# A hybrid attention / DeltaNet / MLP layer: eight modulation rows formed in the MLP stage instead of the output projection, and three query tiles transposed inside the attention

## Chip, cores and metric

The kernel runs on one core of a Trainium2 chip. The metric is the device time of one execution in microseconds (us), taken as the median of several runs. Lower is better.

## What is computed

The reference is one layer of a diffusion backbone for 512 latent tokens (width 1024) with 256 context tokens in front of them. Only the latent stream is returned.

```python
mod_lat = silu(c) @ w_mod + b_mod                      # six rows of 1024: sh1, sc1, g1, sh2, sc2, g2
hx = modulate(rms_norm(x), sh1, sc1)                   # and hc from the context, with its own rows
... = split_cols(hx @ w_in)                            # attention q, k, v; DeltaNet q, k, v; gates
attn_x = latent_attention(q_x, [k_c, k_x], [v_c, v_x]) # 8 query heads, 2 key heads, head width 128
gdn_x  = gdn_output(gdn_bidirectional(...), z_x)       # chunked gated DeltaNet, both directions
x = x + g1 * ((sigmoid(g_a) * (attn_x @ w_pa) + sigmoid(g_d) * (gdn_x @ w_pd)) @ w_out)
x = x + g2 * conv_ffn(modulate(rms_norm(x), sh2, sc2)) # up 1024 -> 5632, conv of width 3, gate, down
return rms_norm(x, final_norm_w)
```

`g2` scales the MLP's output alone, so nothing reads it before the first column block of the down projection is finished.

## The kernel before

Every large product is done in three TensorE passes: both operands are split into a rounded part and the rest (`whi`, `wlo` for weights, `...H`, `...L` for activations), and `mm3` issues hi·hi, hi·lo and lo·hi. So each weight tile of 512 KB is loaded (`load_w`, L205, on the DMA queue of the sync engine, SP), rounded on ScalarE (ACT, L118, tile `whi`) and subtracted on VectorE (DVE, L106, tile `wlo`). `load_w` has two buffers for the raw tile and three each for `whi` and `wlo`.

The stages follow each other on TensorE (PE):

1. Modulation rows sh1 and sc1, normalised inputs, then the attention's k, v and q projections, block by block (`blk`, six of them). A q tile of 128 tokens x 256 columns (two heads) is accumulated in a PSUM tile `pq`, rotated (`rope`, on DVE, which reads `pq`) into an SBUF tile `qt`, and later transposed by `columns` (L89, PSUM tile `pt`, two buffers) into QH (ACT) and QL (DVE). `columns` runs `LAG` = 3 tiles behind the projection, through the list `pend`; the tiles left in `pend` after the last block are transposed in a loop behind it.
2. The attention (`attend`), which goes over 32 pairs of head and token tile. For each it computes scores into the PSUM tile `pS`, the softmax, the transposes of the probabilities (`ab`), and for every second pair the product with the values. Between these steps it takes steps from a generator of projections for the DeltaNet (`fillA`, matmuls into `mb`). A finished projection is transposed by `tokens` through `xbank`, a single PSUM tile named `xb`: ACT copies it out and then takes squares of it in place.
3. The DeltaNet, woven with further projections, with the projection by `w_pa` of the attention's output and, last, with the projection by `w_pd` of the DeltaNet's output. For each of the eight column blocks c, `finish_pd` loads two stored tiles (`gd` and `ga`, L1234 and L1236, two buffers each), multiplies the block's PSUM bank into `gd` on DVE (L115), adds `ga` on GpSimd (POOL, L106), and writes the result to yH (ACT) and yL (DVE, L115, both named `y`).
4. The output projection, `out_proj`: eight column blocks c, each 24 matmuls over k = 0..7 of yH and yL, into PSUM tiles `mc`. Block c = 0 needs the eighth y tile at its last three matmuls.
5. `normed` forms the second normalised input h2 by halves of the tokens, between matmuls; then 44 blocks of the up projection (`up`, `up_finish`), the down projection, and the last normalisation (`emit`, tile `ot`).

`late_mods` is a generator that forms the other four modulation rows g1, sh2, sc2 and g2, 32 steps of 128 entries each. A step loads one 512 KB tile of `w_mod` (L381, tile `wl`, two buffers) and multiplies it on DVE by silu(c), `cw`, with a sum along the row (L382); every eight steps a small add puts eight columns into `mod`. `more_mods(rate)` takes the next step whenever the rates add up to one: 0.25 per k in `w_pa` (MPA), 0.14 in `w_pd` (MPD), 0.25 in `out_proj` (MPO). That is 16 steps in the first, 8 in the second, and the last 8, which are g2, in `out_proj`.

The order on PE is the program's (`pinned[0]` holds it there). On the other engines a scheduler puts instructions in order by priority (`first()`, `sooner()`) and by its own estimate of when they can start, so instructions of a later stage can stand ahead of earlier ones. An engine, and SP's DMA queue too, then works strictly in that order: an instruction that waits holds up all behind it.

Of the kernel before, what the change touches and what calls it, by code (L numbers as in the profile page):

```python
# [45 lines left out]
PMB = 1  # L46
XV, YV = 4, 0
NS = 2
MPA, MPD, MPO = .25, .14, .25
DA = '203242'  # L50
DAT = [(int(DA[i]), int(DA[i + 1])) for i in range(0, len(DA), 2)]
KPIN, LAG, FQ = 1, 3, 0
# [24 lines left out]
def hybrid_layer_body(tc, x, ctxt, xT, consts, cols, rows, w_mod1, w_mod2, w_av, w_aq, w_cm, w_pa, w_pd, w_out,  # L77
# [39 lines left out]
    def act(out, a, f=AF.Copy, **kw):  # L117
        A.activation(out, a, f, **kw)  # L118
# [13 lines left out]
    with es:  # L132
# [61 lines left out]
        def xbank():  # L194
            return xps.tile([P, 4, P], F32, name="xb", tag="x")
# [171 lines left out]
        def late_mods():  # L367
            cw = lmp[0].tile([P, D], F32, name="cw")
            ms = lmp[0].tile([P, 32], F32, name="ms")

            def row():
                return lmp[0].tile([P, D], F32, name="wl", tag="wl", bufs=2)

            SP.dma_start(cw, rows[R_C:R_END].partition_broadcast(P))
            th = row()
            act(th, cw, AF.Tanh, scale=0.5)
            stt(cw, th, 1.0, cw, ALU.add, ALU.mult)
            yield
            for j in range(32):
                wl = row()  # L380
                SP.dma_start(wl, w_mod2[j])  # L381
                tc.keep_in_program_order(V.scalar_tensor_tensor(out=wl, in0=wl, scalar=0.5, in1=cw, op0=ALU.mult, op1=ALU.mult,  # L382
                                                                accum_out=ms[:, j:j + 1]))
                if j % 8 == 7:
                    tt(mod[:, 9 + j:17 + j], ms[:, j - 7:j + 1], col[:, S_BMOD + 9 + j:S_BMOD + 17 + j], ALU.add)
                yield

        lm_es, lmp, mods, mcount = ExitStack(), [], late_mods(), [0.0]

        def more_mods(rate):  # L390
            mcount[0] += rate
            while mcount[0] >= 1:
                mcount[0] -= 1
                next(mods, None)
# [253 lines left out]
        with kv_es:  # L648
# [16 lines left out]
                        tt(o5[:, :, hf, :], s5[:, :, 1 - hf, :], b4[:, :, hf, :], ALU.mult)  # L665
                tt(out, out, tmp, ALU.add)

            def columns(blk, t, qt):
                pt = kps.tile([P, 2, P], F32, name="pt", tag="pt", bufs=2)
                for j in range(2):  # L670
                    transpose(pt[:, j, :], qt[:, j * 128:j * 128 + 128])
                ts_ = slice(t * P, t * P + P)
                hi, lo = (KH, KL) if blk == 0 else (QH[blk - 2], QL[blk - 2])
                split(hi[:, :, ts_], lo[:, :, ts_], pt)
# [4 lines left out]
            for blk in range(6):  # L679
# [5 lines left out]
                for t in range(6 if blk < 2 else 4):  # L685
# [14 lines left out]
                    if blk == 1:  # L700
                        split(VH[:, t, :], VL[:, t, :], pq[:, 0:256])
                        V.tensor_copy(psc[:, t, :], pq[:, 256:288])
                        continue
                    qt = kvp.tile([P, 256], F32, name="qt", tag="qt", bufs=LAG + 1)
                    tmp = kvp.tile([P, 256], F32, name="qtmp", tag="qtmp", bufs=2)
                    if blk == 0:
                        ss = kvp.tile([P, 2], F32, name="kss", tag="kss", bufs=2)
# [21 lines left out]
            chunk[0] = 1  # L729
            for i in range(FQ):  # L730
                next(fillA, None)
            while pend:
                columns(*pend.pop(0))
            pinned[0] = False
        tb_es.close()

# [1 line left out]
        with at_es:  # L738
# [63 lines left out]
            def attend():  # L802
                U = 4 * NH
                at = lambda u: (u // 4, u % 4)
                pS, pms, pv = scores(0, 0), {}, None
                yield F0
                for u in range(U + 2):
                    if u < U:
                        pms[u] = softmax(*at(u), pS)
                    if u + 1 < U:  # L810
                        pS = scores(*at(u + 1))
                    yield F1
                    nxt = None
                    if 0 < u <= U:
                        nxt = probs(*at(u - 1), pms.pop(u - 1))
                    yield F2
                    if pv is not None:
                        pv()
                    yield F3
                    pv = nxt  # L820
# [508 lines left out]
        with ExitStack() as fe:  # L1329
# [40 lines left out]
            def out_proj(c, w, cols):  # L1370
                po = m2bank()[:, cols]
                for k in range(KT):
                    ks = slice(k * P, k * P + P)
                    mm3(po, w[0][:, ks], w[1][:, ks], yt[0][:, k, cols], yt[1][:, k, cols], k, KT)
                    more_mods(MPO)
                with first():
                    stt(x1[c][:, cols], po, mod[:, 16 + c:17 + c], x1[c][:, cols], ALU.mult, ALU.add)

# [65 lines left out]
                            normed(1, token_rows(rc))  # L1444
            for ci in ups[:UH]:
                up_finish(ci)
            for ci in ups[UH:]:
                up(ci, load_w(w_up[ci]), slice(0, NL))
                up_finish(ci)
            pinned[0] = False  # L1450

            fnw = lambda c: col[:, S_FNW + c:S_FNW + c + 1]
# [14 lines left out]

            def emit(i, pr):
                h = half(i)
                ot = fs.tile([P, KT, HT], F32, name="ot", tag="ot")  # L1470
                for j in (KT - 1, *range(KT - 1)):
                    if j == KT - 1:
                        stt(ot[:, j, :], x1[j][:, h], fnw(j), pr, ALU.mult, ALU.mult)
                    else:
                        tt(ot[:, j, :], x1[j][:, h], pr, ALU.mult)
                for (c0, n) in ((KT - 1, 1), (0, 3), (3, 2), (5, 2)):
                    SP.dma_start(outT[c0:c0 + n, :, h].rearrange("c p n -> p c n"), ot[:, c0:c0 + n, :])
# [103 lines left out]
```

## Time and profile before

| | us |
|---|---|
| median of 3 runs | 1266.66 |
| the three runs | 1260.86, 1266.66, 1273.11 |
| the profiled execution, its own time | 1263.61 |
| its span in the trace | 1261.8 |
| PE busy | 1197.7 (95% of the span) |
| DVE busy | 837.8 (66%) |
| ACT busy | 614.1 (49%) |

All times inside the program are counted from the start of the span. The q projections end at about 151 us, the attention runs from there to about 320 us, the DeltaNet with the projections woven into it to about 834 us, the output projection to about 885 us, and the MLP to the end. A busy PE can run at full clock or at half of it; the column PEclk gives the granted clock of a stretch as a share of 2.4 GHz.

### The profile page before, as it was taken

To read this page: it belongs to the slowest core of one execution; us is meant where nothing else is said; L and a number is where in the kernel's file an instruction comes from. 1 tells how busy PE (TensorE), PEld (TensorE's weight loads), DVE (VectorE), ACT (ScalarE), POOL (GpSimd) and SP (SyncE) were. 2 spreads that over 40 slices of the span, in tenths; PEclk is the share of its full clock that TensorE was granted. 3 is DMA by queue.
4 is the path that set the end of the run, shared out by engine and by line. 5 is a ranking of instruction groups with operands and counts; after the bars stand their busy time and mean duration, and the time that the engine had idled before them with its cause. 6 is when DMAs were issued, how large, how long until landed. Compare 5 with 4: busy or idle time off the path is not lost.

```text
span 1261.8 us, 20507 instructions
## 1 busy us (share of the span) xinstructions
PE 1197.7 (95%) x7733; PEld 1017.9 (81%) x7733; DVE 837.8 (66%) x1608; ACT 614.1 (49%) x1402; POOL 276.9 (22%) x347
## 2 busy tenths in 40 slices
PE   7999899999878999999999989899999999999997
PEld 4599889899767788778888778679988888888886
DVE  5667767777699866866657777866765566653333
ACT  6534476666766663763635532223544444442231
POOL 0030110110432496596484100220000000000000
PEclk8999999999999999999999999989999999999998
DMA  9312311121636434444436776883133332233331
GB/s 380 138 59 84 103 42 68 71 76 59 204 110 196 158 126 141 137 146 141 147 124 206 260 262 203 270 309 117 51 100 100 100 101 94 90 96 95 102 93 67
DMA packets 66323, 171.31 MB, mean 136 GB/s; under 512 B 7376, under 2 KB 18096, under 8 KB 64816
## 3 DMA queue, kind: packets, MB, share of 16 engines
q1 hardware_dynamic: 66224, 170.00, 40.4%
q8 instruction: 61, 1.00, 0.3%
q14 instruction: 38, 0.31, 0.1%
HBM read 144.75 MB, written 25.21 MB: 135 GB/s over the span
## 4 chain that ended last, share of the span: by engine, by line
PE 72%; DVE 9%; DMA 8%; POOL 4%; ACT 4%; issue 3%; SPq 0%; POOLq 0%; DVEq 0%; ACTq 0%
PE mc L85 32%; PE mb L85 17%; PE pq L85 6%; PE pb L85 5%; PE pS L85 3%; PE ab L85 3%; DMA wl<-in_w_mod_dram 2%; DVE wlo L106 2%; PE pm L85 2%; PE ab L89 2%; DMA Gb<-gamdr 1%; POOL prod L106 1%; POOL R L106 1%; POOL NN L106 1%; PE pk L85 1%
## 5 line engine op out<-in xcount | busy, mean ns | idle before, releaser
L106 DVE TENSOR_TENSOR wlo<-wraw,whi 128x1024 fp32r<-128x1024 f32 (+1 forms) x153 | 192.7, 1260 | 159.1 <-ACT whi L118 158.2
L118 ACT ACTIVATE whi<-wraw 128x1024 fp32r<-128x1024 f32 (+1 forms) x153 | 159.7, 1044 | 215.0 <-PE mc L85 109.0
L85 PE MATMUL mc<-h,whi 128*128 128x512 f32 (+1 forms) x752 | 219.7, 376 | 0.3 <-ACT whi L118 0.3
L85 PE MATMUL mb<-hxH,whi 128*128 128x512 f32 x384 | 161.4, 420 | 5.4 <-DVE t L115 2.7
L85 PEld LDWEIGHTS mc<-h,whi 128*128 128x128 f32 x752 | 138.0, 188 | 26.1 <-ACT whi L118 0.5
L85 PE MATMUL mb<-hxH,wlo 128*128 128x512 f32 x384 | 151.3, 394 | 0.0
L85 PE MATMUL mb<-hxL,whi 128*128 128x512 f32 x384 | 150.8, 393 | 0.0
L85 PE MATMUL mc<-h,wlo 128*128 128x512 f32 (+1 forms) x376 | 141.3, 376 | 0.5 <-DVE wlo L106 0.5
L85 PE MATMUL mc<-a,whi 128*128 128x512 f32 (+1 forms) x396 | 111.1, 366 | 0.6 <-DVE x L115 0.6
L106 POOL TENSOR_TENSOR rc<-rc,mhalf 128x2 f32<-128x2 f32 x4 | 3.0, 745 | 411.5 <-DVE rc L112 411.5
L85 PEld LDWEIGHTS mb<-hxH,wlo 128*128 128x128 f32 x384 | 72.5, 189 | 16.6
L85 PEld LDWEIGHTS mb<-hxH,whi 128*128 128x128 f32 x384 | 72.9, 190 | 15.8 <-issue 3.6
L85 PEld LDWEIGHTS mc<-a,whi 128*128 128x128 f32 x396 | 71.5, 189 | 12.8 <-DVE x L115 0.8
L85 PEld LDWEIGHTS mc<-h,wlo 128*128 128x128 f32 x376 | 70.8, 188 | 13.6 <-DVE wlo L106 1.0
L85 PEld LDWEIGHTS mb<-hxL,whi 128*128 128x128 f32 x384 | 73.1, 190 | 9.6
L85 PE MATMUL mc<-a,wlo 128*128 128x512 f32 (+1 forms) x198 | 72.3, 365 | 0.0
L115 DVE SCALAR_TENSOR_TENSOR u<-mc,col,u 128x511 f32<-128x511 f32 x88 | 65.3, 746 | 1.4
L106 POOL TENSOR_TENSOR R<-R,prod 128x31 f32<-128x31 f32 (+15 forms) x93 | 58.1, 625 | 7.0
L106 POOL TENSOR_TENSOR prod<-X,R 128x31 f32<-128x31 f32 (+15 forms) x93 | 53.3, 573 | 19.9 <-DVE X L106 13.2
L85 PE MATMUL pq<-whi,hxH 128*128 128x256 f32 (+1 forms) x192 | 55.4, 288 | 0.0
L85 PE MATMUL pq<-wlo,hxH 128*128 128x256 f32 (+1 forms) x192 | 54.1, 282 | 0.0
L85 PE MATMUL pq<-whi,hxL 128*128 128x256 f32 (+1 forms) x192 | 54.0, 281 | 0.0
(323 smaller groups left out, 2768.5 us busy)
## 6 DMA issues: line engine op xcount, KB each, us to landing
wraw<-in_w_cm_dram SPq DMA_DIRECT2D x48, 512.0 KB, 3.5
wraw<-in_w_up_dram SPq DMA_DIRECT2D x44, 512.0 KB, 3.3
wl<-in_w_mod_dram SPq DMA_DIRECT2D x32, 512.0 KB, 4.6
wm<-in_w_mod_dram SPq DMA_DIRECT2D x8, 1024.0 KB, 10.3
wraw<-in_w_down_dram SPq DMA_DIRECT2D x16, 512.0 KB, 3.5
wraw<-in_w_aq_dram SPq DMA_DIRECT2D x10, 512.0 KB, 4.2
M<-gamdr SPq DMA_DIRECT2D x64, 64.0 KB, 4.8
wraw<-in_w_pa_dram SPq DMA_DIRECT2D x8, 512.0 KB, 4.6
```

Source lines behind the costliest of these rows:

```text
L85: i = nc.tensor.matmul(*a, **k)
L89: i = nc.tensor.transpose(*a, **k)
L106: (eng or V).tensor_tensor(out=out, in0=a, in1=b, op=op)
L115: V.scalar_tensor_tensor(out=out, in0=a, scalar=s, in1=b, op0=op0, op1=op1)
L118: A.activation(out, a, f, **kw)
```

## The change

Three edits. First, `late_mods` stops after 24 steps, and `out_proj` takes none. The last eight are formed by a new generator, `gate_mods`, in the first MLP stage: it loads c once more (`cw2`), forms silu(c) in two instructions (a tanh on ACT, an `stt` on DVE), then loads the rows two at a time (1 MB each) into the tile `ot`, which `emit` uses at the very end, and multiplies them on DVE, two instructions for each load. It is stepped after every up block with an odd index. Second, `columns` accepts a PSUM tile from outside; the loop that emptied `pend` behind the q projections is gone, and `attend` transposes one of the three remaining q tiles in each of its first three rounds, through `xbank`. Third, `qt` moves to the pool that lives through the attention, and `ot` takes the shape of two rows.

```diff
-MPA, MPD, MPO = .25, .14, .25
+MPA, MPD = .25, .14
@@ late_mods
-            for j in range(32):
+            for j in range(24):
                 wl = row()
...
+        def gate_mods(pool, fs):
+            two_rows = lambda: fs.tile([P, 2, D], F32, name="wl2", tag="ot")
+            cw = pool.tile([P, D], F32, name="cw2")
+            ms = pool.tile([P, 8], F32, name="ms2")
+            SP.dma_start(cw, rows[R_C:R_END].partition_broadcast(P))
+            th = two_rows()
+            act(th[:, 0], cw, AF.Tanh, scale=0.5)
+            stt(cw, th[:, 0], 1.0, cw, ALU.add, ALU.mult)
+            yield
+            for j in range(0, 8, 2):
+                wl = two_rows()
+                SP.dma_start(wl, w_mod2[24 + j:26 + j].rearrange("j p d -> p j d"))
+                yield
+                for i in range(2):
+                    tc.keep_in_program_order(V.scalar_tensor_tensor(out=wl[:, i], in0=wl[:, i], scalar=0.5, in1=cw, op0=ALU.mult,
+                                                                    op1=ALU.mult, accum_out=ms[:, j + i:j + i + 1]))
+                yield
+            tt(mod[:, 40:48], ms, col[:, S_BMOD + 40:S_BMOD + 48], ALU.add)
@@ columns
-            def columns(blk, t, qt):
-                pt = kps.tile([P, 2, P], F32, name="pt", tag="pt", bufs=2)
+            def columns(blk, t, qt, pt=None):
+                if pt is None:
+                    pt = kps.tile([P, 2, P], F32, name="pt", tag="pt", bufs=2)
@@ the q projections
-                    qt = kvp.tile([P, 256], F32, name="qt", tag="qt", bufs=LAG + 1)
+                    qt = ap_.tile([P, 256], F32, name="qt", tag="qt", bufs=LAG + 1)
...
-            while pend:
-                columns(*pend.pop(0))
             pinned[0] = False
@@ attend
                     yield F1
+                    if pend:
+                        columns(*pend.pop(0), xbank()[:, 0:2, :])
                     nxt = None
@@ out_proj
-                    more_mods(MPO)
@@ the up projection
+            gates = gate_mods(fp, fs)
             for ci in ups[UH:]:
                 up(ci, load_w(w_up[ci]), slice(0, NL))
                 up_finish(ci)
+                if ci % 2:
+                    next(gates, None)
+            for _ in gates:
+                pass
@@ emit
-                ot = fs.tile([P, KT, HT], F32, name="ot", tag="ot")
+                ot = fs.tile([P, 2, D], F32, name="ot", tag="ot").rearrange("p a (b n) -> p (a b) n", n=HT)
```

On PE, at the end of the q projections, the transposes of four q tiles, two each, stand between the last `pq` matmul and the first scores before the change (`pt<-cst,qt`: half a q tile against the identity):

```order
L85 MATMUL pq<-whi,hxL 128x256
L85 MATMUL pq<-wlo,hxH 128x256
L89 MATMUL pt<-cst,qt 128x128 x8
L85 MATMUL pS<-KH,QH_720 128x512
L85 MATMUL pS<-KL,QH_720 128x512
```

Of these eight, two are left there with the change:

```order
L85 MATMUL pq<-whi,hxL 128x256
L85 MATMUL pq<-wlo,hxH 128x256
L89 MATMUL pt<-cst,qt 128x128 x2
L85 MATMUL pS<-KH,QH_720 128x512
L85 MATMUL pS<-KL,QH_720 128x512
```

The other six stand in the first three rounds of the attention. On PE the third of these three tiles is between the transposes of a projection (`xb<-cst,co`) and those of the probabilities (`ab<-cst,pm`), in the same PSUM tile `xb` as the one before it:

```order
L85 MATMUL mb<-hcL,whi 128x256
L85 MATMUL mb<-hcH,wlo 128x256
L89 MATMUL xb<-cst,co 128x128 x2
L89 MATMUL xb<-cst,qt 128x128 x2
L89 MATMUL ab<-cst,pm 128x128 x6
L85 MATMUL mb<-hcH,whi 128x256
```

So the transposes of three tiles moved from a stretch without other matmuls into rounds that have them, and into a bank that others use.

On DVE, where the last `w_pd` blocks end and the output projection begins, before the change (`wl,ms<-wl,cw` is a modulation row, `gd<-gd,mb` and `y<-gd` are the first and last step of `finish_pd`, `x_0<-mc` is the first block of `out_proj`):

```order
L115 SCALAR_TENSOR_TENSOR gd<-gd,mb 128x512 x2
L106 TENSOR_TENSOR wlo<-wraw,whi 128x1024
L382 SCALAR_TENSOR_TENSOR wl,ms<-wl,cw 128x1024
L115 SCALAR_TENSOR_TENSOR y_9122<-gd,y_9122 128x512
L382 SCALAR_TENSOR_TENSOR wl,ms<-wl,cw 128x1024
L115 SCALAR_TENSOR_TENSOR y_9122<-gd,y_9122 128x512
L106 TENSOR_TENSOR wlo<-wraw,whi 128x1024
L382 SCALAR_TENSOR_TENSOR wl,ms<-wl,cw 128x1024
L115 SCALAR_TENSOR_TENSOR gd<-gd,mb 128x512
L382 SCALAR_TENSOR_TENSOR wl,ms<-wl,cw 128x1024
L115 SCALAR_TENSOR_TENSOR gd<-gd,mb 128x512
L106 TENSOR_TENSOR wlo<-wraw,whi 128x1024
```

The same place with the change:

```order
L115 SCALAR_TENSOR_TENSOR gd<-gd,mb 128x512
L106 TENSOR_TENSOR wlo<-wraw,whi 128x1024
L115 SCALAR_TENSOR_TENSOR y_9122<-gd,y_9122 128x512 x2
L106 TENSOR_TENSOR wlo<-wraw,whi 128x1024
L115 SCALAR_TENSOR_TENSOR gd<-gd,mb 128x512
L115 SCALAR_TENSOR_TENSOR y_9122<-gd,y_9122 128x512
L115 SCALAR_TENSOR_TENSOR gd<-gd,mb 128x512
L106 TENSOR_TENSOR wlo<-wraw,whi 128x1024
L115 SCALAR_TENSOR_TENSOR y_9122<-gd,y_9122 128x512
L115 SCALAR_TENSOR_TENSOR x_0_9495<-mc,mod,x_0_9495 128x512
```

The rows between the steps of `finish_pd` are gone, and of its last two blocks, c = 6 now finishes (`y`) ahead of the first step of c = 7.

On SP's DMA queue the 44 loads of the up projection stood in one piece before. With the change c (`cw`) and the four pairs of rows (`wl`, 128x2x1024) stand among them:

```order
L205 DMA wraw<-in_w_up_dram 128x1024 x5
L393 DMA cw_10224<-in_rows_dram 128x1024
L400 DMA wl_10339<-in_w_mod_dram 128x2x1024
L205 DMA wraw<-in_w_up_dram 128x1024 x8
L400 DMA wl_10491<-in_w_mod_dram 128x2x1024
L205 DMA wraw<-in_w_up_dram 128x1024 x4
L400 DMA wl_10643<-in_w_mod_dram 128x2x1024
L205 DMA wraw<-in_w_up_dram 128x1024 x4
L400 DMA wl_10795<-in_w_mod_dram 128x2x1024
L205 DMA wraw<-in_w_up_dram 128x1024 x23
```

Each pair's load has to wait until the pair ahead of it, in the same single tile, has been multiplied, and the weight loads behind it wait with it. On DVE the first pair's two multiplications stand between the eleventh and the twelfth `wlo` of the up projection, and each further pair four `wlo` later. On ACT the tanh of c stands between the sixth and the seventh tile of `normed`'s first half, ahead of the first Silu of the MLP.

## Rows read from the trace of the kernel before

**Rows 1.** The profile page's section 1 (busy us, share of the span, instructions) and the engines' shares of the chain that ended last.
```profile
PE 1197.7 (95%) x7733; PEld 1017.9 (81%) x7733; DVE 837.8 (66%) x1608; ACT 614.1 (49%) x1402; POOL 276.9 (22%) x347
PE 72%; DVE 9%; DMA 8%; POOL 4%; ACT 4%; issue 3%; SPq 0%; POOLq 0%; DVEq 0%; ACTq 0%
```

**Rows 2.** The timeline of PE where the output projection begins: start us, us, line, operation, tiles, count, and in brackets the idle time before it and what ended it.
```profile
833.70 0.63 PE L85 MATMUL mc<-y,whi 128*128 128x512 f32 x2
...
839.91 0.50 PE L85 MATMUL mc<-y,whi 128*128 128x512 f32 x1 [1.59 <-DVE y L115]
841.66 0.80 PE L85 MATMUL mc<-y,whi 128*128 128x512 f32 x1 [0.77 <-DVE y L115]
...
848.24 0.39 PE L85 MATMUL mc<-y,wlo 128*128 128x512 f32 x1
...
848.92 0.39 PE L85 MATMUL mc<-y,wlo 128*128 128x512 f32 x1
```

**Rows 3.** Stretches of the same place: from:to, length, busy us and instructions of PE, PEld, DVE, ACT, POOL, then PEclk, DMA share, GB/s.
```profile
808.00:812.00 4.00, 1.93 (x9) 1.31 (x8) 2.20 (x4) 1.06 (x1) 1.16 (x1) 1.00 1.05 362
841.00:842.00 1.00, 0.34 (x1) 0.34 (x2) 0.61 (x2) 0.00 (x0) 0.00 (x0) 0.50 1.03 385
847.00:848.00 1.00, 1.00 (x4) 0.80 (x3) 0.00 (x0) 0.00 (x0) 0.00 (x0) 0.64 0.99 401
```

**Rows 4.** The timeline of DVE there, as in rows 2.
```profile
823.06 1.89 DVE L106 TENSOR_TENSOR wlo<-wraw,whi 128x1024 fp32r<-128x1024 f32 x1
824.87 2.31 DVE L382 SCALAR_TENSOR_TENSOR wl<-wl,cw 128x1024 f32<-128x1024 f32 x1
...
827.12 0.68 DVE L115 SCALAR_TENSOR_TENSOR y<-gd,y 128x512 fp32r<-128x512 f32 x1
...
832.83 1.23 DVE L382 SCALAR_TENSOR_TENSOR wl<-wl,cw 128x1024 f32<-128x1024 f32 x1 [2.15 <-DMA wl<-in_w_mod_dram]
...
833.99 0.68 DVE L115 SCALAR_TENSOR_TENSOR gd<-gd,mb 128x512 f32<-128x512 f32 x1
```

**Rows 5.** The other steps of `finish_pd`: two rows of ACT's timeline, and of the view of the tile `gd` (count, min/median/max ns, first and last start) its POOL step and, last, the DMA time from issue to landing.
```profile
823.90 0.63 ACT L118 ACTIVATE y<-gd 128x512 fp32r<-128x512 f32 x1 [0.89 <-POOL gd L106]
826.13 0.63 ACT L118 ACTIVATE y<-gd 128x512 fp32r<-128x512 f32 x1 [1.60 <-POOL gd L106]
L106 POOL TENSOR_TENSOR gd<-gd,ga x8: 1294/2199/2305, 797.6 to 837.1; 128x512 f32<-128x512 f32 x8
DMA to landing us min/median/max: 3.7/5.4/5.8
```

**Rows 6.** The timelines of PE and DVE at the end of the q projections, as in rows 2.
```profile
150.61 0.60 PE L89 MATMUL pt<-cst,qt 128*128 128x128 f32 x4
154.33 0.44 PE L89 MATMUL pt<-cst,qt 128*128 128x128 f32 x2 [3.12 <-DVE QL L106]
155.39 0.78 PE L85 MATMUL pS<-KH,QH 128*128 128x512 f32 x1
153.26 0.60 DVE L106 TENSOR_TENSOR qtmp<-pq,qB 128x64 f32<-128x64 f32 x4
```

**Rows 7.** Stretches of the same place, columns as in rows 3.
```profile
154.00:155.00 1.00, 0.44 (x2) 0.20 (x2) 0.93 (x3) 0.20 (x1) 0.91 (x1) 0.91 0.89 188
157.00:158.00 1.00, 1.00 (x6) 0.90 (x5) 0.30 (x1) 0.00 (x0) 0.00 (x0) 0.50 0.08 16
```

**Rows 8.** The timelines of PE and ACT in the first rounds of the attention, where `xb` is used.
```profile
165.69 0.82 PE L89 MATMUL ab<-cst,pm 128*128 128x128 f32 x6
170.09 0.82 PE L89 MATMUL ab<-cst,pm 128*128 128x128 f32 x6
172.21 0.66 PE L89 MATMUL xb<-cst,co 128*128 128x128 f32 x4 [0.59 <-ACT xb L118]
166.00 0.19 ACT L118 ACTIVATION_READ_ACCUMULATOR xb<-xb 128x1 f32 x1
170.29 0.38 ACT L118 ACTIVATE co<-xb 128x256 f32<-128x256 f32 x1 [1.49 <-PE xb L89]
```

**Rows 9.** The second token sums in `normed`: DVE's scale `rc` and the diagonal `dg`, and PE's use of `dg`.
```profile
889.20 0.16 DVE L112 TENSOR_SCALAR rc<-mc 128x2 f32<-128x2 f32 x1
890.36 0.48 DVE L110 TENSOR_SCALAR dg<-cst,rc 128x128 f32<-128x128 f32 x2 [0.59 <-POOL rc L106]
892.34 0.60 PE L85 MATMUL mc<-dg,cst 128*128 128x128 f32 x4
```

**Rows 10.** The MLP's up projection: a stretch of 40 us (columns as in rows 3), and of the waits from 905 to 1080 us (who waited for whom, us in total, times, longest) two rows.
```profile
920.00:960.00 40.00, 40.00 (x178) 33.14 (x177) 24.06 (x30) 17.79 (x23) 0.00 (x0) 1.00 0.30 99
DVE wlo L106 <- ACT whi L118: 55.4, 32, 4.4
PEld mc L85 <- DVE wlo L106: 1.0, 1, 1.0
```

**Rows 11.** The rows of `w_mod` before: the multiplications on DVE (min/median/max ns), the tanh of c on ACT, and the only load of an activation table from there on.
```profile
L382 DVE SCALAR_TENSOR_TENSOR wl<-wl,cw x32: 1210/1219/2316, 709.6 to 854.6; 128x1024 f32<-128x1024 f32 x32
L118 ACT ACTIVATE wl<-cw x1: 1060/1060/1060, 704.0 to 704.0; 128x1024 f32<-128x1024 f32 x1
907.78 1.28 ACT L118 ACT_TABLE_LOAD   x1 [0.83 <-DVE u L115]
```

## The prediction

> **What bounds the kernel now.** I read the page's busy times and chain first: PE is busy for 95% of the span and holds 72% of the chain that ended last [rows 1]. So an edit pays only where PE waits, or runs at half clock. The timeline of PE around the two places that the change touches shows both. Where the output projection begins, PE waits 1.59 us and 0.77 us for DVE's y tiles and then works at half rate: 16 matmuls from 841.66 to 848.24 took 6.58 us, where three from 848.24 to 848.92 took 0.68 [rows 2]. The granted clock there is 0.50, 1.2 GHz, and back at full before 848 [rows 3]. Where the attention begins, PE waits 3.12 us for DVE, and again works at half clock, from about 154.9 to 158.1 [rows 6, 7]. In the MLP's up projection PE has no wait at all and DVE is busy 24.06 of 40 us [rows 10].
>
> **Part one: eight rows leave the output projection.** Removed are eight loads of 512 KB and eight DVE multiplications of 1.21 us at least and up to 2.32 beside POOL [rows 11]. Only those on the path of the last two y tiles (blocks c = 6 and 7 of w_pd) count. That path runs: y of block 4 frees `gd`, its load is issued, lands a median 5.4 us later, then DVE, POOL (1.3 to 2.3), ACT (0.63), DVE (0.68) [rows 4, 5].
> Before: ACT has the hi part of block 4 at 823.90 + 0.63 = 824.53, but DVE runs a row from 824.87 for 2.31 us, and y follows at 827.12. The load for block 6 comes behind that; a further row at 832.83, itself held 2.15 us by its load, puts block 6's first step at 833.99 [rows 4].
> After, with the rows gone: DVE is free at 823.06 + 1.89 = 824.95, y of block 4 ends at 825.6, that of block 5 (ACT done at 826.13 + 0.63 = 826.76) at 827.5. Loads land at 831.0 and 832.9. Block 6: 0.68 + 1.3 + 0.63 + 0.68 from 831.0 gives 834.4. Block 7 stands behind it on DVE: first step to 835.1, POOL up to 2.3 beside a `wlo`, 837.4, ACT 838.0, DVE 838.7. PE starts block 0 of the output projection at 833.70 [rows 2] and needs block 7 after 21 matmuls of 0.227 us, at 838.5. So of 1.59 + 0.77 = 2.36 us about 0.2 stays: 2.2 us gained.
> The half clock: 16 matmuls at 0.227 us are 3.6, so 6.58 - 3.6 = 2.9 us more. The clock fell after two waits close together. The wait of 2.07 us that ends at 810.86 is in a stretch at granted clock 1.00 [rows 3]. So 0.2 us will not bring it down: 2.9 us gained. Together 5.1. Bounds: at best 5.3 (no wait at all); at worst 0, if block 7 arrives as late as now. I take 5.1, since the path holds 3 us of rows and needs only 2.4 us less. What is late next is nothing on PE for the rest of this projection: since three weight tiles are held ready.
>
> **Part two: the same work in the MLP.** Four loads of 1 MB, one of c, a tanh (1.06 us), an stt, and eight multiplications of 1.22 us [rows 11].
> The tanh and the stt fall into `normed`, ahead of the second `rc`. They delay it by about 0.7 us (the stt begins 0.5 us earlier than `rc` does now and takes 1.2). `dg` is now ready at 890.84 and PE uses it at 892.34 [rows 9]: 1.5 us of cover, so no cost; without the cover up to 1.2 us.
> A pair holds DVE for 2.5 us, once in four up blocks. Its cover: in 40 us DVE is idle for 16, and `wlo` waits 55.4 us in 32 times for ACT's rounding, which waits for a buffer to come free, while PE waited for `wlo` once, 1.0 us [rows 10]. A weight tile is ready some two blocks before PE wants it, so a delay of 2.5 us stays hidden. On SP's queue a pair's load waits for the pair ahead, which DVE finishes before the `wlo` that the next weight load waits for anyway. So 0, with a bound of four pairs times 2.5 = 9.8 us if all of it came through, and none below zero, since PE has no wait there to lose.
> One rule speaks against this part. The only table load after the early tanh at 704 is the 1.28 us at 907.78, ahead of the first Silu [rows 11]. The Trainium skill (ScalarE: Activation LUTs, section "Table sets: the hidden batching unit") says that functions should be grouped by table set, because each change of set costs a load. By that rule a tanh behind the first Silu would bring two more loads, and the sum would be 2.6 us higher; in the order the tanh stands ahead of that Silu, under the set that served the tanh at 704, so the sum takes none.
>
> **Part three: three q tiles transposed inside the attention.** The first scores no longer stand behind six transposes. They wait for the last reader of the `pq` bank that they take over: DVE ends it at 153.26 + 0.60 = 153.86, and PE begins 0.1 us later, where it begins at 155.39 now [rows 6]: 1.4 us earlier. PE's idle time is 2.9 us, hardly shorter than now, so I let the clock fall as it does; as more work then runs at half rate, 1.2 us are left.
> What is added lies in `xb`, a single bank: each pair of transposes (0.24 us) waits until ACT has finished with the tile before. In round 2 PE would be at the transposes of the probabilities at 165.69 - 1.0, while the squares of `xb` end at 166.19, some 0.9 earlier by now: 0.6 us of wait. In round 3 the pair stands directly behind a transpose into the same bank, whose copy begins at 170.29 and is followed by two squares of 0.45 us each [rows 8]: PE stands for 1.5 us, with the probabilities behind it. In return the wait of 0.59 us at 172.21, for those same squares, is gone [rows 8]. Sum: -1.2 + 0.7 + 0.6 + 1.5 - 0.6 = 1.0, of which some 0.6 goes in waits that PE has in these rounds anyway: +0.4 us. Bounds: -3.0, if the clock stays up (1.6 us more) and no wait arises; +2.7, if ACT, which gets three more copies into its fullest rounds, makes the two waits twice as long. I take +0.4, by the order of the rows.
>
> **Sum.** -5.1 + 0 + 0.4 = -4.7 us. The profiled execution took 1263.61 us, which gives 1258.9. It lies 3.05 us below the median of the runs shown, and the runs spread over 12; for a median I add half of that difference: 1260.4 us.
>
> **Rivals.**
> The wait stays (B): block 7 is late for another reason, its load or POOL's add, and PE stands again for 1.5 us and loses its clock. For it: the load's landing takes up to 5.8 us [rows 5], and the x tiles are loaded in the same stretch at a DMA share of 1.03 [rows 3]. Against: these loads are issued two microseconds earlier, before that burst. Gain about 1 us, less 0.4: 1263 us, or 1264.5 as a median.
> The MLP is starved (C, the slower side): the pairs come through to PE. Place: the `wlo` behind each pair; price 2.5 us for each, 9.8 in all; it decides from the point where a weight tile is ready less than 2.5 us ahead of its block. For it: PE did wait for a `wlo` once, at the head of this stage. Against: that was before the three buffers had filled, and none followed [rows 10]. 1258.9 + 9.8 = 1268.7, slower than the profiled execution by 5 us; 1270 as a median.
> The attention keeps its clock (D): an idle time of 2.9 us lies between the 2.07 that did not bring the clock down and the 3.12 that did [rows 3, 6]. Then this part gives up to 3.0 instead of costing 0.4: 1255.5, or 1257 as a median.
>
> **How the numbers follow.** Forecast 0.53, B 0.22, C 0.10, D 0.15. The range: D's 1255.5 less 3 us, as far as the lowest of the runs lies below the profiled one, is 1252.5; C's 1270 and 1 us is 1271. A measurement of this kernel tells about 1% from no change, 12.7 us. Faster by that means under 1254, which only the lower tails of D and of the forecast reach: 0.09. Slower by that needs C together with the bad end of the attention and a half clock in the MLP: 0.04. The rest, 0.87, is the same.
>
> **What would show it.** Right: no `y` wait of over 0.5 us on PE around 834 to 845 and a granted clock of 1.00 there; the first scores about 1.4 us earlier, then a wait of PE of about 1.5 us at the third `xb<-cst,qt`; PE without a wait beside the four pairs; `rc` about 0.7 us later with PE unmoved. Wrong: a wait of PE on `wlo` in the up projection, a half clock at the head of the output projection, a second table load in the MLP, or an attention that ends more than 3 us later or earlier against its beginning than now.

## Result and profile after

| | before | after |
|---|---|---|
| median, us | 1265.78 (1260.86 to 1273.11, 20 runs) | 1259.17 (1254.90 to 1264.39, 20 runs) |
| the profiled execution, us | 1263.61 | 1254.90 |
| its span, us | 1261.8 | 1253.1 |

The ratio is 0.9948 with a 95% interval of 0.9935 to 0.9961: 6.6 us faster, between 4.9 and 8.2. That is a change of less than 1%, to which the prediction gave a chance of 0.87. The time that it forecast, 1260.4 us, is 1.2 above the measured median.

The profile page of the changed kernel, section 1 and the engines' shares of the chain that ended last [rows 1]:

```profile
PE 1193.0 (95%) x7733; PEld 1015.7 (81%) x7733; DVE 834.0 (67%) x1609; ACT 613.8 (49%) x1403; POOL 274.0 (22%) x347
PE 74%; DMA 7%; DVE 6%; POOL 5%; ACT 4%; issue 2%; SPq 0%; POOLq 0%; DVEq 0%; ACTq 0%
```

The work is the same; PE's busy time shrank by 4.7 us, 3.6 of them from 820 to 848 us, since a matmul at half clock counts as busy for longer. The two profiled executions differ by 8.7 us, more than the medians. To see where, the same matmul in PE's order is looked up in both traces, and the table gives by how much a stretch between two such matmuls is longer (+) or shorter (-) than in the trace of before, in us. The bounds are times in the trace of before; the runs are those of the experiments below.

| kernel | 0-150 | 150-200 | 200-330 | 330-395 | 395-760 | 760-820 | 820-848 | 870-890 |
|---|---|---|---|---|---|---|---|---|
| after | +2.3 | +0.24 | 0.0 | -0.6 | -3.9 | -0.3 | -6.43 | 0.0 |
| a2, after again | 0.0 | +0.23 | +0.1 | +0.7 | -0.8 | -0.5 | -6.30 | 0.0 |
| e1, rows only | +1.6 | -0.05 | 0.0 | +3.5 | -0.5 | +0.2 | -6.59 | 0.0 |
| e2, transposes only | +1.9 | +0.22 | 0.0 | +2.8 | -0.8 | -0.4 | -0.81 | 0.0 |
| e4, rows late | +0.1 | 0.0 | +0.1 | +1.4 | -2.0 | +0.5 | -3.08 | +3.70 |
| f0, rows and loads late | +0.1 | 0.0 | +0.1 | +3.5 | -0.1 | 0.0 | -6.54 | +6.63 |
| e8, rows narrow | +0.4 | 0.0 | +0.1 | +3.7 | -0.8 | +0.2 | -4.20 | 0.0 |
| f1, after + two loads | +2.1 | +0.22 | 0.0 | -1.1 | -3.0 | +0.4 | -5.07 | 0.0 |
| f2, after + multiplications | +2.4 | +0.19 | 0.0 | +4.0 | -1.8 | -0.4 | -4.27 | 0.0 |
| e5, other bank | +2.6 | -1.14 | +0.1 | +2.5 | -4.7 | +0.5 | -6.36 | 0.0 |
| e6, clock kept | +1.8 | -0.73 | 0.0 | +3.5 | +1.5 | +2.1 | -6.49 | 0.0 |
| c1, e5 and e6 | +0.2 | -2.04 | 0.0 | +2.2 | -0.6 | +0.5 | -6.54 | 0.0 |
| e7, more MLP work | +2.4 | +0.17 | +0.1 | +2.4 | -3.2 | -0.5 | -6.17 | 0.0 |

From 848 to 870 every run is within 0.01 us of before, and from 890 to 1250 within 0.04; behind that up to 0.5 us is left out here. In the stretches 0-150 and 330-760 PE has the work of before in all of these kernels, and yet they differ by several us. The edits are not the cause of all that: after and a2 are the same program, and differ by 2.3, 1.3 and 3.1 us in 0-150, 330-395 and 395-760; and e1, e4, f0 and e8, in which DVE, ACT and POOL work in the order of before from 330 to 395, are 1.4 to 3.7 us longer there. (In the kernels with the moved transposes a few instructions of DVE and ACT stand in another order in these stretches; what that is worth was not tried.) The stretches that the edits touch are steadier: kernels with the same code agree to 0.2 us from 150 to 200, and the eight without rows and loads at the head of the output projection agree to 0.4 us from 820 to 848. With the stop still there the spread is larger: e2 has the code of before from 820 to 848 and takes 0.81 us less. So effects are read by stretch here, and the change's gain in this one is 6.4 us against the profiled execution of before, 5.6 against e2.

**The output projection.** PE's timeline where it begins (start us, us, line, operation, tiles, count), and a stretch of 11 us (from:to, length, busy us and instructions of PE, PEld, DVE, ACT, POOL, then PEclk, DMA share, GB/s) [rows 2, 3]:

```profile
830.67 0.61 PE L85 MATMUL mc<-y,whi 128*128 128x512 f32 x2
...
834.75 0.62 PE L85 MATMUL mc<-y,whi 128*128 128x512 f32 x2
835.20 0.39 PE L85 MATMUL mc<-y,wlo 128*128 128x512 f32 x1
835.43 0.79 PE L85 MATMUL mc<-y,whi 128*128 128x512 f32 x2
...
839.48 0.39 PE L85 MATMUL mc<-y,wlo 128*128 128x512 f32 x1
```
```profile
834.00:845.00 11.00, 11.00 (x50) 8.86 (x49) 5.62 (x8) 4.99 (x8) 0.27 (x1) 1.00 0.52 173
```

No wait is left and the granted clock is 1.00: from 830.67 to 839.48 it takes 8.8 us, where before the same matmuls (833.70 to 848.24) took 14.5. DVE's timeline behind it, then SP's queue (gd's loads) and two rows of the view of the tile `gd` (count, min/median/max ns, first and last start) [rows 4, 5]:

```profile
817.82 0.69 DVE L115 SCALAR_TENSOR_TENSOR gd<-gd,mb 128x512 f32<-128x512 f32 x1 [0.24 <-DMA gd<-tdr]
819.85 0.69 DVE L115 SCALAR_TENSOR_TENSOR gd<-gd,mb 128x512 f32<-128x512 f32 x1 [1.26 <-PE mb L85]
822.98 1.28 DVE L115 SCALAR_TENSOR_TENSOR y<-gd,y 128x512 fp32r<-128x512 f32 x2
827.89 0.69 DVE L115 SCALAR_TENSOR_TENSOR gd<-gd,mb 128x512 f32<-128x512 f32 x1 [0.44 <-DMA gd<-tdr]
834.97 0.69 DVE L115 SCALAR_TENSOR_TENSOR y<-gd,y 128x512 fp32r<-128x512 f32 x1 [1.84 <-ACT y L118]
```
```profile
814.37 0.92 SPq L1255 DMA_DIRECT2D gd<-tdr  x2
823.68 0.93 SPq L1255 DMA_DIRECT2D gd<-tdr  x2
```
```profile
L106 POOL TENSOR_TENSOR gd<-gd,ga x8: 1288/1300/2276, 795.5 to 832.1; 128x512 f32<-128x512 f32 x8
DMA to landing us min/median/max: 3.4/4.1/5.9
```

The last y ends at 834.97 + 0.69 = 835.66, and PE takes it in the pair that starts at 835.43. It comes just in time: nothing is to spare. And gd lands in 4.1 us at the median, where it took 5.4.

**The attention.** PE's rows at its head, with what ended their waits, and a stretch there [rows 6 to 8]:

```profile
156.31 0.77 PE L85 MATMUL pS<-KH,QH 128*128 128x512 f32 x1 [3.02 <-DVE qsc L112]
167.37 0.44 PE L89 MATMUL xb<-cst,qt 128*128 128x128 f32 x2 [0.54 <-ACT xb L118]
173.15 0.44 PE L89 MATMUL xb<-cst,qt 128*128 128x128 f32 x2 [1.27 <-ACT xb L118]
```
```profile
157.00:158.00 1.00, 1.00 (x5) 0.82 (x4) 0.00 (x0) 0.00 (x0) 1.00 (x1) 0.50 0.74 250
```

Against matmuls ahead of it, which run 2.3 us later in this execution, the first scores come 1.4 us earlier (156.31 - 155.39 - 2.3). The profile names `qsc` as what ended their wait; it stands on DVE right behind the last reader of `pq`, which ends at 156.17, and the two are not told apart. Then two waits for ACT's last use of `xb` follow, and the 1.4 us are gone. The clock falls to a half as before.

**The MLP.** DVE and PE in `normed`, the up projection's first 40 us, the new multiplications, and ACT's one table load [rows 9 to 11]:

```profile
881.00 0.15 DVE L112 TENSOR_SCALAR rc<-mc 128x2 f32<-128x2 f32 x1
883.58 0.61 PE L85 MATMUL mc<-dg,cst 128*128 128x128 f32 x4
```
```profile
920.00:960.00 40.00, 40.00 (x178) 33.15 (x177) 28.79 (x39) 16.29 (x21) 0.00 (x0) 1.00 0.43 148
L403 DVE SCALAR_TENSOR_TENSOR wl<-wl,cw x8: 1217/1219/1224, 929.2 to 995.6; 128x1024 f32<-128x1024 f32 x8
899.02 1.28 ACT L118 ACT_TABLE_LOAD   x1 [0.83 <-DVE u L115]
```

`rc` stands 2.58 us ahead of PE's use of `dg`, before 3.14: 0.56 us later, and PE unmoved. DVE has 4.7 us more work in these 40, and PE is busy for all of them. The tanh of c under the table in force brought no load.

### The profile page after: what moved, and what is told of

Same layout as the page of the kernel before. It is cut to its first block, busy times and chain, and to the rows that moved or that the text cites. A ratio compares the mean times of both kernels' runs of the same rounds, so it can differ in the third digit from the quotient of the medians.

```text
span 1253.1 us, 20509 instructions
## 1 busy us (share of the span) xinstructions
PE 1193.0 (95%) x7733; PEld 1015.7 (81%) x7733; DVE 834.0 (67%) x1609; ACT 613.8 (49%) x1403; POOL 274.0 (22%) x347
## 4 chain that ended last, share of the span: by engine, by line
PE 74%; DMA 7%; DVE 6%; POOL 5%; ACT 4%; issue 2%; SPq 0%; POOLq 0%; DVEq 0%; ACTq 0%
PE mc L85 33%; PE mb L85 19%; PE pq L85 6%; PE pb L85 5%; PE pS L85 3%; PE ab L85 3%; PE pm L85 2%; PE ab L89 2%; DVE wlo L106 1%; POOL NN L106 1%; DMA NN<-gamdr 1%; POOL prod L106 1%; DMA Gb<-gamdr 1%; POOL R L106 1%; PE pk L85 1%
```

## Experiments

Ratios are to the kernel before, with 95% intervals. Edits are shown against the kernel named.

**e1, the rows alone** (before with the first edit; shown against after).

```diff
+            while pend:
+                columns(*pend.pop(0))
...
-                    if pend:
-                        columns(*pend.pop(0), xbank()[:, 0:2, :])
```

> The kernel before with the first edit alone: the eight g2 rows move to the MLP, the three q tiles stay transposed behind the q projections. My theory (the change's gain is the path of the last two y tiles and the half clock behind it): about 5 to 6 us faster than before, the PE position at the output projection's first full block about 6 us earlier against the last w_pd block than before, and the first scores where they were. Rival (the attention edit carries a part of the 8.7 us between the two profiled executions): 3 us or less.

Ratio 0.9948 (0.9927 to 0.9968), as the whole change; 820 to 848 is 6.59 us shorter. So the gain is the moved rows'.

**e2, the transposes alone** (before with the second edit; shown against after).

```diff
-            for j in range(24):
+            for j in range(32):
...
+                    more_mods(MPO)
...
-                if ci % 2:
-                    next(gates, None)
```

> The kernel before with the second edit alone: the three q tiles transposed inside the attention, the g2 rows still in the output projection. My theory: -0.5 to +0.5 us, first scores 1.3 us earlier, and that given back by 175 us in two waits of PE at xb. The stop at the output projection is as before: waits of 1.6 and 0.8 us and a half clock of 6 us. Rival (the attention edit is worth something): 1.5 us faster or more, with PE still ahead at 300 us.

Ratio 0.9986 (0.9966 to 1.0005); +0.22 us from 150 to 200, with the two `xb` waits of 0.54 and 1.27 us of the changed kernel, and around the start of the output projection this:

```profile
826.96 0.70 PE L85 MATMUL mb<-g_s,whi 128*128 128x512 f32 x2 [1.10 <-DVE gd L115]
844.75 0.59 PE L85 MATMUL mc<-y,whi 128*128 128x512 f32 x1 [2.17 <-DVE y L115]
846.50 0.80 PE L85 MATMUL mc<-y,whi 128*128 128x512 f32 x1 [0.30 <-DVE y L115]
```

The stop is still there, but not in the sizes expected: waits of 1.10, 2.17 and 0.30 us, and a half clock of some 3.5 us (granted clock 0.50 from 845 to 848) instead of 6. Before has 0.44, 1.59 and 0.77 us and some 6.5 us of half clock in the same code, so both vary between executions. The transposes cost 0.2 us in their stretch; by the whole time, within its interval, no change.

**e4, the rows late in the output projection** (against before).

```diff
-                    more_mods(MPO)
+                    more_mods(MPO if c > 3 else 0)
```

> The kernel before with one edit: the eight g2 rows stay in the output projection, with their loads, but start only in its column block 4, behind the last y tile, not at block 0. Theory (the rows cost only because they stand between the steps of the last two w_pd blocks on DVE and in front of their loads): the same 5 to 6 us gained as by moving them to the MLP, less up to 1 us at the end of this projection, where DVE takes rows between the last x tiles. Rival (the stage is short of DVE time or of DMA as a whole, wherever the rows stand in it): 2 us or less gained, with new waits of PE on x tiles or weights later in the projection.

Ratio 0.9997 (0.9981 to 1.0013): nothing gained, a miss for my theory as stated. The stretches show two reasons: only 3.08 us come off at the head, and 3.70 are lost at the end. PE's waits in this run, three around the head and two at the end, then the granted clock behind the fourth:

```profile
823.60 0.71 PE L85 MATMUL mb<-g_s,whi 128*128 128x512 f32 x2 [1.31 <-DVE gd L115]
840.79 0.49 PE L85 MATMUL mc<-y,whi 128*128 128x512 f32 x1 [1.11 <-ACT y L118]
841.52 0.50 PE L85 MATMUL mc<-y,whi 128*128 128x512 f32 x1 [0.23 <-DVE y L115]
876.26 0.38 PE L85 MATMUL mc<-cst,acc 128*128 128x1 f32 x2 [1.03 <-DVE acc L106]
882.36 0.71 PE L85 MATMUL mc<-dg,cst 128*128 128x128 f32 x4 [0.59 <-DVE dg L110]
```
```profile
879.00:881.00 2.00, 2.00 (x11) 2.00 (x10) 1.49 (x3) 0.00 (x0) 0.00 (x0) 0.50 0.00 0
```

At the end DVE has rows between the squares' sums (`acc`) that PE waits for. At the head no row is on DVE any more, and gd and y are late all the same: two of the rows' loads still stand on SP's queue ahead of gd and ga, since their tiles are free. f0, below, takes these away.

**e8, the rows narrow** (against before: 8 columns of 1024 in the eight multiplications, loads as they were).

```diff
+                n = D if j < 24 else 8
-                tc.keep_in_program_order(V.scalar_tensor_tensor(out=wl, in0=wl, scalar=0.5, in1=cw, ...
+                tc.keep_in_program_order(V.scalar_tensor_tensor(out=wl[:, 0:n], in0=wl[:, 0:n], scalar=0.5, in1=cw[:, 0:n], ...
```

> The kernel before, with the loads of the eight g2 rows where they are, but each of their DVE multiplications over 8 columns instead of 1024, so the sum of g2 leaves out 1016 of 1024 terms. This takes away DVE's time for the rows and leaves their transfers and the waits for them. If DVE's time is what makes the last y tiles late: 5 us gained or more. If the wait for the rows' loads (2.15 us of DVE at 832.83) or the transfers' share of the DMA engines is: 2 us or less, with PE's waits of over 1 us for y still there. My theory has both on the path: about 3 us gained, and a stop for block 6 or 7 of under 1.5 us left.

Ratio 0.9976 (0.9958 to 0.9994); 4.20 us off the stretch, with waits of 1.08 and 0.23 us for y left. Both sides seem to be on the path; f1 and f2 part them.

**f1, the changed kernel with two of the loads back** (in `late_mods`, stepped from block 0 of `out_proj`).

```diff
+            for j in (24, 25):
+                SP.dma_start(row(), w_mod2[j])
+                yield
```

> The changed kernel, with only the loads of two rows put back where the first two of the moved ones stood before: on SP's queue ahead of the gd loads of blocks 4 and 5 and ahead of the ga loads of blocks 6 and 7. Their data are not used, and no multiplication comes back. Theory T (the two loads hold up gd and ga: behind them gd landed in 5.0 to 6.0 us, without them in under 4): gd's first step at block 4 comes 1.5 to 2 us later against the PE order, PE waits about 1 us for y at the output projection with a half clock behind it, 3 to 4 us slower than the changed kernel. Theory D (DVE's time for the rows made y late, as the prediction has it): within 0.5 us of the changed kernel, no wait for y.

Ratio 0.9976 (0.9956 to 0.9995); 5.07 us off the stretch instead of 6.43. SP's queue, DVE's first step of blocks 4 and 5, and PE:

```profile
814.13 0.33 SPq L388 DMA_DIRECT2D wl<-in_w_mod_dram  x1
814.73 0.93 SPq L1258 DMA_DIRECT2D gd<-tdr  x2
```
```profile
819.96 1.51 DVE L115 SCALAR_TENSOR_TENSOR gd<-gd,mb 128x512 f32<-128x512 f32 x2 [1.26 <-DMA gd<-tdr]
837.29 0.50 PE L85 MATMUL mc<-y,whi 128*128 128x512 f32 x1 [0.41 <-ACT y L118]
838.02 0.51 PE L85 MATMUL mc<-y,whi 128*128 128x512 f32 x1 [0.23 <-DVE y L115]
```

Behind one load of 512 KB, gd's first step starts 5.2 us after the issue at 814.73, instead of 3.5 (814.37 to 817.82). PE stops twice for y, but no half clock follows:

```profile
837.00:843.00 6.00, 5.48 (x23) 4.34 (x24) 3.07 (x5) 1.98 (x4) 0.00 (x0) 1.00 0.72 245
```

The cost is 6.43 - 5.07 = 1.4 us and not the 3 to 4 expected.

**f2, the changed kernel with the eight multiplications back, without loads.**

```diff
+            for j in range(24, 32):
+                wl = row()
+                tc.keep_in_program_order(V.scalar_tensor_tensor(out=wl, in0=cw, scalar=0.5, in1=cw, op0=ALU.mult, op1=ALU.mult,
+                                                                accum_out=ms[:, j:j + 1]))
+                yield
```

> The changed kernel, with only the eight multiplications put back on DVE at their old places in the output projection, on data that are in SBUF already, so without any load. Their sums are not used. Theory D (DVE's time for the rows makes y late): PE waits for y for 1.5 us or more at the output projection, then a half clock, 4 to 6 us slower than the changed kernel. Theory T (the loads do it): PE waits under 0.5 us, within 1.5 us of the changed kernel.

Ratio 0.9983 (0.9965 to 1.0001); 4.27 us off the stretch. PE's one wait, DVE ahead of it, and the clock behind it:

```profile
843.97 0.50 PE L85 MATMUL mc<-y,whi 128*128 128x512 f32 x1 [1.92 <-DVE y L115]
```
```profile
839.85 2.31 DVE L389 SCALAR_TENSOR_TENSOR wl<-cw 128x1024 f32<-128x1024 f32 x1
842.09 1.22 DVE L389 SCALAR_TENSOR_TENSOR wl<-cw 128x1024 f32<-128x1024 f32 x1
843.24 1.28 DVE L115 SCALAR_TENSOR_TENSOR y<-gd,y 128x512 fp32r<-128x512 f32 x2
```
```profile
845.00:846.00 1.00, 1.00 (x6) 0.78 (x5) 0.52 (x1) 0.76 (x1) 0.00 (x0) 1.00 0.51 197
```

Two rows run on DVE while the last y tiles wait for it. The multiplications alone cost 6.43 - 4.27 = 2.2 us and not the 4 to 6 expected; again no half clock. Two loads alone cost 1.4 (f1). Before, with both, there were 3.4 us of stops (below), after which the clock did fall.

**f0, rows and loads late** (against before; e4, and each tile gets a column of a finished x tile first).

```diff
+                if j >= 24:
+                    V.tensor_copy(wl[:, 0:1], late[0])
                 SP.dma_start(wl, w_mod2[j])
```

> The kernel with the eight rows late in the output projection (as the earlier run with late rows), whose loads now also wait: each tile gets one column copied from a finished x tile before its load, so that no load of these rows stands ahead of gd or ga. If the early loads are what was left of the stop in the earlier run: no wait for y of over 0.4 us, no half clock, and the stretch 820 to 848 us 6 to 6.5 us shorter than before, where the earlier run had 3.1. If something else held y: 3 to 4 us again. At the end of the projection (870 to 890) 3 us or more are lost, since the rows, now later still, stand between the last x tiles.

The stretch is 6.54 us shorter, with no wait for y (PE busy for all of 11 us) and granted clock 1.00:

```profile
836.00:847.00 11.00, 11.00 (x50) 9.05 (x49) 6.64 (x8) 3.50 (x6) 1.29 (x1) 1.00 0.83 285
```

So multiplications and early loads are the whole cause. How much each takes is less sure. Against e4 the loads alone make 6.54 - 3.08 = 3.5 us here, where two loads in the same places made 1.4 in f1; the narrow rows of e8, with all eight loads, lie between (6.54 - 4.20 = 2.3). The difference is in gd's landing too (PE waited 1.31 us for it in e4, and less than 0.1 in f1); why was not tried. And 870 to 890 is 6.63 us longer, so the ratio is 0.9986 (0.9955 to 1.0017). Neither end of the output projection has room for these rows.

**e7, more work beside the pairs** (against after).

```diff
+                    for _ in range((0, 1, 3, 7)[j // 2]):
+                        tc.keep_in_program_order(V.scalar_tensor_tensor(out=wl[:, i], in0=wl[:, i], scalar=0.0, in1=wl[:, i],
+                                                                        op0=ALU.mult, op1=ALU.add))
```

> The changed kernel with the DVE work beside the four pairs of rows made larger step by step: before each multiplication 0, 1, 3 and 7 more of the same shape that leave the row as it is, so the pairs hold DVE for about 2.4, 4.9, 9.8 and 19.5 us. If a weight tile is ready some two blocks ahead, as the prediction has it (a block of 24 matmuls by 0.227 is 5.4 us): the first two pairs cost PE nothing, the third at most 1 us, the fourth 6 to 12 us. If the cover is less than one block (the starved MLP of the rivals): the second pair already stops PE.

Not even the fourth pair costs anything: 890 to 1250 is unchanged. A stretch of 40 us within it:

```profile
1000.00:1040.00 40.00, 40.00 (x178) 33.12 (x177) 39.94 (x47) 16.18 (x22) 0.00 (x0) 1.00 0.30 95
```

DVE is busy for 39.94 of 40 us and PE for all 40. My 6 to 12 us for the fourth pair were wrong: I had its 19.5 us in one piece, but the scheduler put the weight tiles' `wlo` between them. So DVE's idle time in the stage was cover enough here, and the lead of one weight tile set no limit. The ratio, 0.9969 (0.9947 to 0.9991), is within reach of the changed kernel's.

**e5, the other bank, and e6, the clock kept** (each against after).

```diff
-                        columns(*pend.pop(0), xbank()[:, 0:2, :])
+                        columns(*pend.pop(0), abank().rearrange("p (a b) -> p a b", b=P)[:, 0:2, :])
```
```diff
+                warm = xbank()
+                for i in range(22):
+                    transpose(warm[:, i % 4, :], ident)
                 pS, pms, pv = scores(0, 0), {}, None
```

> The changed kernel, with the three q tiles of the attention transposed through the bank rotation ab instead of the single tile xb. If PE's waits there (0.54 us at 167.4 and 1.27 us at 173.2) come from xb's last readers on ACT: both are gone or under 0.3 us, and the PE position at 175 us is 1 to 2 us earlier against the first scores. If ACT and DVE are late in these rounds whatever the bank: waits of the same size at the probabilities' transposes, which use ab too, and no change.

> The changed kernel, with 22 transposes of the identity into the free xb tile, results not used, on PE between the last q transposes and the first scores, where it is idle for 3.0 us now and then works at half clock for some 3 us. If the idle time brings the clock down and PE waits for nothing else there: granted clock 1.00 from 156 to 160, the attention's PE position 1.5 us earlier behind it, 1.0 to 1.6 us faster than the changed kernel. If the work saved goes into PE's waits in the first attention rounds: the lead is gone by 175 us, and no change.

e5: ratio 0.9954 (0.9937 to 0.9971); the `xb` waits for q tiles are gone, waits of 0.21 and 0.25 us stand further on, and 150 to 200 is 1.4 us shorter than in the changed kernel. e6: ratio 0.9970 (0.9953 to 0.9987); that stretch is 1.0 us shorter. The clock there:

```profile
157.00:158.00 1.00, 1.00 (x6) 0.82 (x5) 0.88 (x2) 0.00 (x0) 0.51 (x1) 1.00 0.86 299
```

It is 1.00 where the changed kernel had 0.50; the two `xb` waits, 0.55 and 1.27 us, stay, and PE, ahead by now, waits 0.34 us for ACT at 159.52. The idle time is what brought the clock down: in all kernels but e6 and c1 PE is idle there for 3.02 to 3.12 us, and the granted clock is at 0.50 within a microsecond of the end of it, in e5 too; in these two it stays at 1.00.

**c1, both, and a2, the changed kernel again** (c1 is e6 with e5's edit and this one; a2 has no edit).

```diff
-                for i in range(22):
+                for i in range(26):
```

> The changed kernel with both attention edits: the three q tiles through the rotation ab, and 26 identity transposes (results not used) on PE in its idle time before the first scores. By the two runs alone, which moved the stretch from 150 to 200 us by -1.4 and -1.0 us against the changed kernel, the sum is -2 to -2.5 us in that stretch, if the waits removed and the clock kept are separate; if the work that comes earlier only meets the next waits, -1.4 or less. From 400 us on it is the changed kernel, so 2 us faster than that and 8 us faster than before, or nothing seen if later stretches differ from run to run by more than that.

> The changed kernel itself, beside the combined one on the same chip: ratio to before 0.993 to 0.997. By stretches: 820 to 848 us 6.4 us shorter than before, whatever the rest of the run does; the stretch 330 to 395, whose code is that of before, anywhere from 1 us shorter to 4 us longer, as in the runs so far.

c1: ratio 0.9953 (0.9933 to 0.9974), median 1259.64 us; a2: 0.9957 (0.9938 to 0.9976), median 1261.69. From 150 to 200 c1 is 2.3 us shorter than the changed kernel, so the two effects add up. The whole times do not tell 2.3 us apart: the profiled c1 has +2.2 us from 330 to 395 in a part that no edit touches.

## Why the prediction was right

**Part one, -5.1 predicted, -6.4 measured.** The mechanism held: the rows are off the path of the last y tiles, the stop goes and the half clock with it. The size was off in one term, the wait taken away, put at 2.2 us; the bound of 5.3 at best was passed. Rows of PE's timeline of before that I had not used:

```profile
821.75 0.39 PE L85 MATMUL mb<-g_k,wlo 128*128 128x512 f32 x1
822.58 0.70 PE L85 MATMUL mb<-g_s,whi 128*128 128x512 f32 x2 [0.44 <-DVE gd L115]
...
837.83 0.50 PE L85 MATMUL mc<-y,whi 128*128 128x512 f32 x1
...
840.50 0.40 PE L85 MATMUL mc<-y,whi 128*128 128x512 f32 x1
```

A start normally follows the last by 0.23 us. By the starts PE lost 839.91 - 837.83 - 0.23 = 1.9 and 841.66 - 840.50 - 0.23 = 0.9 us at the two stops [rows 2], where the idle time in brackets, which I summed, has 2.36 in all; and 822.58 - 821.75 - 0.23 = 0.6 at a stop for gd that I left out. The 0.2 us of wait that I expected to stay did not. So the wait is 3.4 us; with the half clock's 2.9 in this trace, 6.3. In e2's trace of the same code the stops by starts are 4.3 us and the half clock only some 1.4, so the two terms are those of one execution and not of the kernel. The working kept the landing of gd at 5.4 us. It fell to 4.1, since the rows' own loads were ahead of it; these are priced at 1.4 us by f1 and at 3.5 by f0 against e4, DVE's time at 2.2 by f2. I had given nearly all of it to DVE.

**Part two, 0 predicted, 0 measured.** 890 to 1250 us is unchanged, `rc` came 0.56 us later (0.7 expected) under its cover. The rule of the Trainium skill ("ScalarE: Activation LUTs", section "Table sets: the hidden batching unit"), that functions are best grouped by table set, does not speak against this order: with the tanh ahead of the first Silu the trace has one table load there, as before. No run has the tanh behind a Silu, so the prediction's other case, two more loads and 2.6 us, is not tested.

**Part three, +0.4 predicted, +0.24 measured** (+0.23 and +0.22 in a2 and e2). The first scores came 1.4 us earlier (1.4 expected, of which 1.2 were to remain), the waits at `xb` were 0.54 and 1.27 us (0.6 and 1.5 expected), the clock fell.

**From execution to median.** The profiled execution of the changed kernel, 1254.9 us, was the lowest of its 20 runs; its stretch 395 to 760 was 3.9 us shorter than before's, where a2, the same program, has 0.8. The step to the median of half a difference was a choice that worked, not one that the profile backs. That the time came within 1.2 us is in part luck: the gain was put 1.9 us too small (4.7 for 6.6), and the starting point 0.6 too low (1265.1 for 1265.78), which took some of that back.

**The rivals.** The wait stays: refuted in e1 and after. The MLP starved: refuted, with far more work, in e7. The attention keeps its clock: it did not; e6 shows what that is worth, 1.0 us, where 1.6 was reckoned; a wait of 0.34 us for ACT takes some of it there.

## What to carry over

When rows of work move out of a stage, price their loads apart from their arithmetic: a load that is early because its buffer is free can hold up the one that the path waits for. A place is free when the engine is idle there and nothing due soon stands behind, which a run with several times the work shows quickly. Where unchanged stretches differ by more than the effect, compare the stretch itself between the same two instructions.

## What the runs showed of the hardware

Which stop brings TensorE's clock down is not told by the longest wait alone. In f2 a wait of 1.92 us left it at 1.00, and before the change 1.59 and 0.77 us within two us brought 0.50, as did 2.17 and 0.30 in e2; 1.11 and 0.23 in e4 did not. At the end of e4's projection a wait of 1.03 us at 876.26 and eight matmuls of one column were followed by 0.50 from 878.1 on. What decides stays open here.

The same work differs by execution: from 330 to 395 us between -1.1 and +4.0 against before. One wait and the clock around it in f2, then the same time in the changed kernel, whose engines work in the same order there:

```profile
349.26 1.11 PE L89 MATMUL xb<-cst,co 128*128 128x128 f32 x4 [3.31 <-DVE co L115]
```
```profile
345.00:355.00 10.00, 6.69 (x36) 6.45 (x35) 6.57 (x5) 9.25 (x27) 3.39 (x2) 0.66 0.32 84
```
```profile
345.00:355.00 10.00, 7.61 (x53) 6.64 (x53) 7.16 (x9) 8.93 (x28) 2.75 (x2) 1.00 0.17 55
```

In f2 PE waited 3.31 us there and the granted clock of these 10 us was 0.66, in the changed kernel the wait was 1.31 and the clock 1.00. Why the wait differs between executions was not tried.
